# MLP, output projection and first gate as seven block products for eight

## The chip, the cores and the metric

The kernel runs on one core of one Trainium2 chip. The metric is device time in microseconds, from runs of the whole kernel. A core has TensorE (matrix products, PE in the profile), VectorE (DVE), ScalarE (ACT), GpSimd (POOL) and SyncE (SP, which here only issues DMAs).

## The reference

Two layers on 1024 tokens of width 1024, in float32. Each layer normalises h, projects it, runs eight heads of forgetting attention and eight of chunkwise retention, and then:

```python
        h = h + mixed @ w_out[i]                                  # 1024 x 1024
        h = h + gated_conv_ffn(rms_norm(h, ffn_norm_w[i]), w_up[i], conv_w[i], conv_b[i], w_down[i])
        gate = jax.nn.sigmoid(rms_norm(h, ple_norm_w[i]) @ w_ple_gate[i])   # 1024 x 1024
        h = h + gate * (p[i] @ w_ple_proj[i])
...
def gated_conv_ffn(u, w_up, conv_w, conv_b, w_down):
    up = u @ w_up                                                 # 1024 x 5632
    a, g = up[..., :D_FF], up[..., D_FF:]                         # D_FF = 2816
    a = causal_depthwise_conv(a, conv_w, conv_b)                  # three taps along the tokens
    return (jax.nn.gelu(a, approximate=False) * g) @ w_down       # 2816 x 1024
```

A final norm follows the second layer.

## The kernel before

Activations lie with features on the 128 partitions and the 1024 tokens along the free axis, so h is eight tiles of 128 x 1024. Each float32 operand is split into a high and a low part of reduced mantissa (`split`: ScalarE writes the high part, VectorE or GpSimd subtracts it from the source). A product of a 128 x 128 block of weights with 512 tokens is three matrix products: high by high, high by low, low by high (`mm_fm`, L163 and L165, two halves of the tokens, so six for a block).

Weights come one load of 512 KB ahead of their use (`load_w`, `fetch`, `weights`; tags wr, wh and wl with two buffers each), in the order that `weight_order` writes out by hand. The engine that makes a low part is read from the strings in `ENGINES`.

A layer runs in this order. First the attention stage: `weave` mixes dense products with attention units by spans written out by hand. Then the output projection: eight column chunks of eight blocks each; h[m] gains the result from PSUM (L738), `make_u` splits the scaled h[m] for the MLP, and its squares join the sum for the norm (`Stats`). Then the MLP: `up` takes one chunk of 128 of the 2816 features, convolves, applies gelu and multiplies with its gate; after every second chunk `down` adds that pair's product into all eight h tiles, by halves of 512 tokens (L780). Then the gate: eight chunks, whole for the first layer, by two pieces of 512 tokens for the last (L847 to L849), with the final norm behind them. `finish` turns the sums of squares into 1 / rms, by small products.

One SBUF pool `sb` and one PSUM pool `ps` serve the whole kernel; tags give the number of buffers (`BUFS`). PSUM has two double banks "d" and four single banks "s". Order on each engine comes from the framework's scheduler, which takes the program order as priority and a timing model of its own for what is ready.

## Time and profile before

| | us |
|---|---|
| median of 3 runs | 2913.52 |
| lowest and highest | 2911.53, 2914.69 |
| span of the profiled execution | 2907.6 |

The span runs from the first to the last instruction of one profiled execution; the run's time holds 5.9 us more at its median. Busy shares are those of the span. In rows, `x2048` counts instructions, `128x512` is partitions by elements, and "idle before" is the idle time of that engine just before such an instruction, with what ended it. A matrix product's own duration overlaps with its neighbours', so the pace is read from start to start. In windows, each engine's busy time is followed by its instruction count; PEclk is the granted TensorE clock as a share of 2.4 GHz.

### The profile page before, as it was taken

The numbers are of one execution on the slowest core, as the hardware profiler recorded it, in microseconds if no ns is written. First come the engines' busy times: TensorE is split into PE (matmuls) and PEld (weight loads), VectorE is DVE, ScalarE is ACT, GpSimd is POOL, SyncE is SP. The second block draws the span as 40 slices with busy tenths as digits, with TensorE's granted clock in tenths as the row PEclk, the third lists the DMA queues.
The fourth block names the chain that finished last, engine by engine and source line by source line (L and its number), as shares of the span: only waits on it lengthen the run. The fifth ranks groups of instructions, "written<-read, shape, count | busy, mean of one in ns | idle before, by whom it ended". The sixth has DMA issues, their size and how long they took to land. (4 is left out here: it accounts for less than half of the span.)

```text
span 2907.6 us, 35602 instructions
## 1 busy us (share of the span) xinstructions
PE 2855.6 (98%) x14654; PEld 2414.9 (83%) x14654; DVE 1559.9 (54%) x2343; ACT 936.6 (32%) x1312; POOL 363.3 (12%) x317
## 2 busy tenths in 40 slices
PE   9999999999999999999999999999999999999998
PEld 8888889888888888888888888888888888888876
DVE  4566655544444445446636666645344445444477
ACT  4455533421211212123435545243221211111243
POOL 2222332200000000000122222321000000000011
PEclk9999999999999999999999999999999999999999
DMA  5234222311111111112343341233111111111123
GB/s 167 83 86 107 57 69 75 141 47 48 51 44 51 46 49 51 44 51 80 117 113 83 88 109 32 71 109 110 44 51 44 51 44 51 47 49 46 60 85 137
DMA packets 70226, 209.79 MB, mean 72 GB/s; under 512 B 8624, under 2 KB 13232, under 8 KB 70064
## 3 DMA queue, kind: packets, MB, share of 16 engines
q1 hardware_dynamic: 66992, 199.12, 22.3%
q10 hardware_dynamic: 3072, 8.39, 1.2%
q8 instruction: 115, 1.88, 0.3%
q14 instruction: 47, 0.39, 0.0%
HBM read 157.09 MB, written 16.84 MB: 60 GB/s over the span
## 5 line engine op out<-in xcount | busy, mean ns | idle before, releaser
L163 PE MATMUL d<-uh,wh 128*128 128x512 f32 x2048 | 644.9, 395 | 0.3 <-ACT uh L100 0.3
L165 PE MATMUL d<-uh,wl 128*128 128x512 f32 x2048 | 639.5, 393 | 2.6 <-POOL wl L97 2.5
L163 PE MATMUL d<-ul,wh 128*128 128x512 f32 x2048 | 640.3, 393 | 0.6 <-DVE ul L101 0.6
L96 ACT CAST wh<-wr 128x1024 fp32r<-128x1024 f32 x232 | 243.2, 1049 | 1117.9 <-PE d L163 611.3
L165 PEld LDWEIGHTS d<-uh,wl 128*128 128x128 f32 x2048 | 384.3, 188 | 88.6 <-POOL wl L97 4.2
L163 PEld LDWEIGHTS d<-ul,wh 128*128 128x128 f32 x2048 | 384.4, 188 | 85.9 <-DVE ul L101 1.0
L163 PEld LDWEIGHTS d<-uh,wh 128*128 128x128 f32 x2048 | 381.3, 188 | 80.9 <-ACT uh L100 0.5
L780 DVE TENSOR_TENSOR h<-s,h 128x512 f32<-128x512 f32 x352 | 233.5, 686 | 173.4 <-PE s L165 171.7
L163 PE MATMUL s<-zh,wh 128*128 128x512 f32 x704 | 258.7, 394 | 0.0
L165 PE MATMUL s<-zh,wl 128*128 128x512 f32 x704 | 258.2, 394 | 0.0
L163 PE MATMUL s<-zl,wh 128*128 128x512 f32 x704 | 258.0, 393 | 0.0
L97 DVE TENSOR_TENSOR wl<-wr,wh 128x1024 fp32r<-128x1024 f32 x176 | 215.9, 1227 | 43.4 <-ACT wh L96 34.8
L183 PE MATMUL d<-wh,uh 128*128 128x256 f32 (+1 forms) x768 | 222.6, 290 | 11.7 <-DVE ks L332 8.6
L184 PE MATMUL d<-wl,uh 128*128 128x256 f32 (+1 forms) x768 | 220.6, 287 | 0.1
L185 PE MATMUL d<-wh,ul 128*128 128x256 f32 (+1 forms) x768 | 219.4, 287 | 0.0
L753 DVE TENSOR_TENSOR a<-d,rb 128x1024 f32<-128x1024 f32 x44 | 53.9, 1224 | 261.0 <-PE d L165 243.0
L762 DVE TENSOR_TENSOR z<-d,rb 128x1024 f32<-128x1024 f32 x44 | 53.9, 1225 | 246.2 <-PE d L165 246.2
L97 POOL TENSOR_TENSOR wl<-wr,wh 128x1024 fp32r<-128x1024 f32 (+1 forms) x56 | 137.4, 2455 | 354.4 <-ACT wh L96 241.1
L752 POOL MEMSET a<- 128x2 f32 x44 | 4.4, 100 | 1386.7 <-DVE zl L97 1268.3
L183 PEld LDWEIGHTS d<-wh,uh 128*128 128x128 f32 x768 | 147.2, 192 | 16.0 <-DVE ks L332 10.3
L165 PEld LDWEIGHTS s<-zh,wl 128*128 128x128 f32 x704 | 132.3, 188 | 31.1
L163 PEld LDWEIGHTS s<-zl,wh 128*128 128x128 f32 x704 | 132.4, 188 | 30.6
(196 smaller groups left out, 4202.0 us busy)
## 6 DMA issues: line engine op xcount, KB each, us to landing
wr<-in_wup_dram SPq DMA_DIRECT2D x88, 512.0 KB, 3.5
wr<-in_wdown_dram SPq DMA_DIRECT2D x44, 512.0 KB, 3.6
wr<-in_wqk_dram SPq DMA_DIRECT2D x32, 512.0 KB, 3.5
wr<-in_wgate_dram SPq DMA_DIRECT2D x24, 512.0 KB, 3.6
wr<-in_wtm_dram SPq DMA_DIRECT2D x20, 512.0 KB, 3.7
ka<-kh SPq DMA_DIRECT2D x32, 256.0 KB, 4.9
kb<-kl SPq DMA_DIRECT2D x32, 256.0 KB, 5.2
yb<-cum_rows SPq DMA_DIRECT2D x16, 512.0 KB, 5.1
```

What stands on the lines that cost most here:

```text
L96: nc.scalar.copy(dst_hi, src)
L97: (eng or nc.vector).tensor_tensor(dst_lo, src, dst_hi.bitcast(F32), op=ALU.subtract)
L163: nc.tensor.matmul(outs[h], whi, x[:, h * 512:(h + 1) * 512], start=s, stop=False)
L165: nc.tensor.matmul(outs[h], wlo, xhi[:, h * 512:(h + 1) * 512], start=False, stop=stop)
L183: nc.tensor.matmul(o, x[k][0][:, tok], hi, start=start, stop=False)
L184: nc.tensor.matmul(o, x[k][0][:, tok], lo, start=False, stop=False)
L185: nc.tensor.matmul(o, x[k][1][:, tok], hi, start=False, stop=stop)
L752: nc.gpsimd.memset(a[:, 0:2], 0.0)
L753: nc.vector.tensor_tensor(a[:, 2:], ad, rb, op=ALU.mult)
L762: nc.vector.tensor_tensor(z, gd, rb, op=ALU.mult)
L780: nc.vector.tensor_tensor(hs, outs[i], hs, op=ALU.add)
```

## The change

The output projection, both parts of the MLP and the gate of the first layer are computed by Strassen's form, in Winograd's variant, with blocks of two by two: weights in four blocks of 128 x 128 (two halves of a pair of K chunks, two halves of a pair of output chunks), activations in four blocks of 128 x 512 (two K chunks, two halves of the tokens). Seven block products, named b0, a, b1, c1, b2, c2 and b3, replace eight. Three PSUM banks hold them: b goes on adding to its bank after each reading out, as does c2 to c1's.

`Moving` holds a pair of activation chunks: the parts that are used as they are and four sums (`sums`), each split in high and low. `Fixed` holds a unit of weights (n pairs of K chunks, one pair of output chunks): GpSimd makes four sums, ScalarE and VectorE split seven blocks; `Line` loads one unit ahead and `parts` spreads its four steps over the products of the unit before. `join` adds block products to h, `form` builds a new tile.

The output projection runs in two halves of K, so units of n = 2. The MLP runs in two stages: all 22 chunks go up, in units of n = 4, and z and its sums go to DRAM (`zd`); then h is read again and the pairs of chunks come back in four groups, units of n = 3, 3, 3 and 2. Pools are opened by stage (`turn_to`): a tile of a new pool waits for the tiles of the old one that lay in its memory, and PSUM in the MLP stages is eight single banks. The last gate is as before, but its weights and `make_u` start in a new pool, as do those of the next attention stage.

```diff
+GROUPS = ((0, 1, 2), (3, 4, 5), (6, 7, 8), (9, 10))
...
-    sb = ctx.enter_context(tc.tile_pool(name="sb", bufs=1))
-    ps = ctx.enter_context(tc.tile_pool(name="ps", bufs=1, space=PSUM))
...
-    BUFS = dict(st=6, tp=5, L=4, c=3, u=16, mh=9)
+    BUFS = dict(st=6, tp=5, L=4, c=2, u=16, mh=9, ssq=1, x=28, wr=4, ws=2, wh=4, wl=3)
+    KEPT = ("mh", "ssq")
+    sb = ps = banks = None
+    @contextmanager
+    def phase(name):
+        nonlocal sb, ps, banks
+        banks = 8 if name[:3] == "ffn" else 4
+        with ExitStack() as stack:
+            sb = stack.enter_context(tc.tile_pool(name="sb_" + name, bufs=1, reuse_waits="tile"))
+            ps = stack.enter_context(tc.tile_pool(name="ps_" + name, bufs=1, space=PSUM, reuse_waits="tile"))
+            yield
...
+            yield from (None, None)
+            for i in range(len(PIECES) if l + 1 == DEPTH else 0):
+                yield from [(ap["wlast"][0, m], KC, P, E("gate%d" % l, i * KC + m)) for m in range(KC)]
...
+    class Moving:
+        def __init__(self, a, b, scales=None, ta=None, tb=None):
+            a1, b1, b2 = a[:, 0:512], b[:, 0:512], b[:, 512:T]
+            if ta is None:
+                ta, tb = sums(a, b, scales)
+            self.x = []
+            for n, (src, scale) in enumerate(((a[:, 0:512], scales and scales[0]), (b[:, 0:T], scales and scales[1]),
+                                              (ta.rearrange("p c t -> p (c t)"), None), (tb.rearrange("p c t -> p (c t)"), None))):
+                if n == 0:
+                    t = G("x", "xs", F32R, (P, 2, 512))
+                    hi, lo = t[:, 0, :], t[:, 1, :]
+                else:
+                    hi, lo = G("x", "xh", F32R), G("x", "xl", F32R)
+                if scale is None:
+                    split(hi, lo, src)
+                else:
+                    split_scaled(hi, lo, src, scale)
+                self.x.append((hi, lo))
+        def of(self, part):
+            n, slot = ((0, 0), (1, 0), (2, 0), (2, 1), (3, 0), (1, 1), (3, 1))[part]
+            return [v[:, slot * 512:(slot + 1) * 512] for v in self.x[n]]
+    def sums(a, b, scales=None):
+        a1, a2, b1, b2 = a[:, 0:512], a[:, 512:T], b[:, 0:512], b[:, 512:T]
+        ta, tb = G("c", "ta", F32, (P, 2, 512)), G("c", "tb", F32, (P, 2, 512))
+        t2, t1, t3, t4 = ta[:, 0, :], ta[:, 1, :], tb[:, 0, :], tb[:, 1, :]
+        if scales:
+            sa, sbb, sn = scales
+            nc.scalar.activation(t3, a2, AF.Copy, scale=sa)
+            nc.vector.scalar_tensor_tensor(t1, a1, sa, t3, op0=ALU.mult, op1=ALU.subtract)
+            nc.vector.scalar_tensor_tensor(t3, b2, sbb, t3, op0=ALU.mult, op1=ALU.subtract)
+        else:
+            sn = -1.0
+            nc.vector.tensor_tensor(t1, a1, a2, op=ALU.subtract)
+            nc.vector.tensor_tensor(t3, b2, a2, op=ALU.subtract)
+        nc.vector.scalar_tensor_tensor(t2, b2, sn, t1, op0=ALU.mult, op1=ALU.subtract)
+        nc.vector.scalar_tensor_tensor(t4, b1, sn, t2, op0=ALU.mult, op1=ALU.subtract)
+        return ta, tb
+    class Fixed:
+        def __init__(self, src, n, loads):
+            self.n, self.w = n, n * P
+            self.raw = []
+            for i in range(2):
+                t = G("wr", "wr", F32, (P, 2, self.w))
+                loads.append(nc.sync.dma_start(t, src[i]))
+                self.raw.append(t)
+            self.x = []
+            self.todo = [self.first, self.second, self.third, self.fourth]
+        def step(self):
+            if self.todo:
+                self.todo.pop(0)()
+        def split(self, t, c=2):
+            if c == 2:
+                hi, lo = G("wh", "wh", F32R, (P, 2, self.w)), G("wl", "wl", F32R, (P, 2, self.w))
+            else:
+                both = G("wh", "wb", F32R, (P, 2, self.w))
+                hi, lo = both[:, 0:1, :], both[:, 1:2, :]
+            nc.scalar.copy(hi, t)
+            nc.vector.tensor_tensor(lo, t, hi.bitcast(F32), op=ALU.subtract)
+            self.x.append((hi, lo))
+        def first(self):
+            self.split(self.raw[0])
+        def second(self):
+            (a, b), s = self.raw, G("ws", "ws", F32, (P, 2, self.w))
+            nc.gpsimd.tensor_tensor(s[:, 1, :], b[:, 0, :], b[:, 1, :], op=ALU.add)
+            nc.gpsimd.tensor_tensor(s[:, 0, :], s[:, 1, :], a[:, 0, :], op=ALU.add)
+            self.p = s
+            self.split(s)
...
+        def take(self):
+            now = self.ahead
+            while now.todo:
+                now.step()
+            self.load()
+            return now
...
+    def parts(line, moving, evac):
+        w = line.take()
+        b, c = bank(), None
+        for part, name in enumerate(("b0", "a", "b1", "c1", "b2", "c2", "b3")):
+            if name == "a":
+                o = bank()
+            elif name == "c1":
+                o = c = bank()
+            else:
+                o = c if name == "c2" else b
+            more = name in ("b1", "b2", "b3", "c2")
+            for p, x in enumerate(moving):
+                whi, wlo = w.of(part, p)
+                xhi, xlo = x.of(part)
+                first, last = p == 0 and not more, p == len(moving) - 1
+                nc.tensor.matmul(o, whi, xhi, start=first, stop=False, skip_group_check=more)
+                nc.tensor.matmul(o, whi, xlo, start=False, stop=False, skip_group_check=more)
+                nc.tensor.matmul(o, wlo, xhi, start=False, stop=last, skip_group_check=more)
+            evac(name, o)
+            if part in (1, 3, 5, 6):
+                line.step()
+    def join(name, s, to):
+        c11, c12, c21, c22 = to[0][:, 0:512], to[0][:, 512:T], to[1][:, 0:512], to[1][:, 512:T]
+        for dst, op in {"b0": [(c11, ALU.add)], "a": [(c11, ALU.add)], "b1": [(c12, ALU.add)], "c2": [(c12, ALU.add)],
+                        "c1": [(c22, ALU.subtract)], "b2": [(c22, ALU.subtract)], "b3": [(c21, ALU.subtract)]}[name]:
+            nc.vector.tensor_tensor(dst, dst, s, op=op)
+    def form(name, s, to, scale):
+        c11, c12, c21, c22 = to[0][:, 0:512], to[0][:, 512:T], to[1][:, 0:512], to[1][:, 512:T]
+        if name in ("b0", "b1"):
+            nc.scalar.copy(c11 if name == "b0" else c12, s)
+        elif name == "c1":
+            nc.scalar.activation(c22, s, AF.Copy, scale=-1.0)
+        elif name in ("a", "c2"):
+            dst = c11 if name == "a" else c12
+            nc.vector.tensor_tensor(dst, dst, s, op=ALU.add)
+        elif name == "b2":
+            nc.vector.tensor_tensor(c22, c22, s, op=ALU.subtract)
+        else:
+            nc.vector.scalar_tensor_tensor(c21, s, -1.0, scale, op0=ALU.mult, op1=ALU.mult)
...
+        line = Line(specs())
+        h = [None] * KC
+        stats = Stats()
+        u = []
+        hs_dram = dr.tile([KC, P, T], F32, name="hs")
+        mx = [Moving(mixed[2 * p], mixed[2 * p + 1]) for p in range(4)]
+        for half in range(2):
+            for q in range(4):
+                if half == 0:
+                    for m in (2 * q, 2 * q + 1):
+                        h[m] = G("mh", "h")
+                        with tc.issue_after(line.loads[0].ins):
+                            nc.sync.dma_start(h[m], h_dram[m])
+                to = h[2 * q:2 * q + 2]
+                parts(line, mx[2 * half:2 * half + 2], lambda name, s: join(name, s, to))
+                if half:
+                    u.append(Moving(*to, scales(2 * NW_FFN + l, q)))
+                    for m in (2 * q, 2 * q + 1):
+                        stats.add(h[m], G("mh", "hsq"))
+                        nc.sync.dma_start(hs_dram[m], h[m])
+        zd = [dr.tile([4, P, T], F32, name="zd%d" % j, bufs=1) for j in range(FC // 2)]
+        rb = None
+        for j in range(FC // 2):
+            act = []
+            body = [G("mh", "a") for i in range(2)]
+            def evac_a(name, s):
+                nonlocal rb
+                if rb is None:
+                    _, rb = stats.finish()
+                form(name, s, body, rb[:, 0:512])
+                if name == "b2":
+                    nc.vector.tensor_tensor(body[1][:, 512:T], body[1][:, 512:T], rb[:, 512:T], op=ALU.mult)
+                elif name == "c2":
+                    nc.vector.tensor_tensor(body[0], body[0], rb, op=ALU.mult)
+            parts(line, u, evac_a)
...
+                for tap in (1, 0):
+                    late = c[:, 2 - tap:T]
+                    nc.vector.scalar_tensor_tensor(late, body[i][:, 0:T - 2 + tap], cw[:, tap:tap + 1], late, op0=ALU.mult, op1=ALU.add)
+                nc.scalar.activation(c, c, AF.Gelu)
+                nc.vector.tensor_tensor(c, c, rb, op=ALU.mult)
+                act.append(c)
...
+            parts(line, u, evac_g)
+            ta, tb = sums(*z)
+            for n, t in enumerate((z[0], z[1], ta.rearrange("p c t -> p (c t)"), tb.rearrange("p c t -> p (c t)"))):
+                nc.sync.dma_start(zd[j][n], t)
...
+        for group in GROUPS:
+            mx = []
+            for j in group:
+                t = []
+                for n, shape in enumerate(((P, 512), (P, T), (P, 2, 512), (P, 2, 512))):
+                    t.append(G("c" if n else "mh", "zz", F32, shape))
+                    src = zd[j][n]
+                    if n == 0:
+                        src = src[:, 0:512]
+                    elif n > 1:
+                        src = src.rearrange("p (c t) -> p c t", c=2)
+                    nc.sync.dma_start(t[-1], src)
+                mx.append(Moving(t[0], t[1], ta=t[2], tb=t[3]))
+            u = []
+            for q in range(4):
+                to = h[2 * q:2 * q + 2]
+                parts(line, mx, lambda name, s: join(name, s, to))
+                if group is GROUPS[-1]:
+                    if l + 1 < DEPTH:
+                        u.append(Moving(*to, scales(2 * NW_PLE + l, q)))
+                    for m in (2 * q, 2 * q + 1):
+                        stats.add(h[m], G("mh", "hsq"), None, E("hsq", m))
...
+            turn_to("attn%d" % (l + 1))
+            fetch()
...
+    turn_to("last")
+    fetch()
+    fetch()
+    u = [make_u(h[m], nw[:, 2 * NW_PLE + DEPTH - 1, m:m + 1]) for m in range(KC)]
```

Left out: comments; `third` and `fourth` of `Fixed` (two more sums by GpSimd, the last two splits); `evac_g` (as `evac_a`, with the activated half as scale); the gate of the first layer (four units of n = 4 by `parts` and `form`, the product with the embedding on GpSimd); the new layout of the weights on the host. In the attention stage `cs` takes the `ssq` buffer.

## Rows read from the trace of the kernel before

**Rows 1.** The page, part 1: busy time, share of span, instructions, by engine.

```profile
PE 2855.6 (98%) x14654; PEld 2414.9 (83%) x14654; DVE 1559.9 (54%) x2343; ACT 936.6 (32%) x1312; POOL 363.3 (12%) x317
```

**Rows 2.** Busy time by stage: window, length, engines, PEclk, DMA share, GB/s.

```profile
545.00:634.00 89.00, 88.45 (x384) 70.86 (x383) 39.12 (x33) 26.79 (x27) 5.52 (x3) 1.00 0.17 54
634.00:1362.00 728.00, 728.00 (x3177) 594.86 (x3178) 362.06 (x385) 159.77 (x150) 6.26 (x23) 1.00 0.15 50
1362.00:1460.00 98.00, 98.00 (x445) 80.88 (x444) 60.88 (x47) 40.06 (x39) 17.54 (x7) 1.00 0.35 118
...
1985.00:2073.00 88.00, 87.47 (x385) 70.43 (x384) 38.06 (x32) 27.45 (x27) 5.33 (x3) 1.00 0.18 54
2073.00:2803.00 730.00, 729.39 (x3177) 595.23 (x3177) 364.80 (x385) 161.08 (x150) 11.05 (x25) 1.00 0.16 50
2803.00:2907.00 104.00, 90.16 (x441) 74.96 (x439) 73.13 (x106) 36.17 (x51) 16.99 (x9) 0.95 0.38 129
```

**Rows 3.** TensorE, groups of instructions by form.

```profile
L163 PE MATMUL d<-uh,wh 128*128 128x512 f32 x2048 | 644.9, 395 | 0.3 <-ACT uh L100 0.3
...
L163 PE MATMUL s<-zh,wh 128*128 128x512 f32 x704 | 258.7, 394 | 0.0
...
L163 PE MATMUL d<-mxh,wh 128*128 128x512 f32 x256 | 80.2, 397 | 1.0 <-DVE h L738 1.0
```

**Rows 4.** The last gate: TensorE by time, then busy sums of 2825 to 2885.

```profile
2842.78 0.39 PE L848 MATMUL d<-ul,wh 128*128 128x512 f32 x1
2843.01 0.39 PE L849 MATMUL d<-uh,wl 128*128 128x512 f32 x1
...
sum 60.00, PE 60.00 PEld 49.34 DVE 48.32 ACT 23.88 POOL 11.18; mean PE 10.00 PEld 8.22 DVE 8.05 ACT 3.98 POOL 1.86
```

**Rows 5.** VectorE in order of time: joins of MLP down, then the first gate.

```profile
698.63 1.88 DVE L780 TENSOR_TENSOR h<-s,h 128x512 f32<-128x512 f32 x3
...
1438.31 1.22 DVE L97 TENSOR_TENSOR wl<-wr,wh 128x1024 fp32r<-128x1024 f32 x1
1439.44 1.28 DVE L101 SCALAR_TENSOR_TENSOR ul<-h,nw,uh 128x1024 fp32r<-128x1024 f32 x1
1440.63 1.22 DVE L811 TENSOR_TENSOR sg<-sg,ppt 128x1024 f32<-128x1024 f32 x1
```

**Rows 6.** ScalarE, groups of instructions by form.

```profile
L96 ACT CAST wh<-wr 128x1024 fp32r<-128x1024 f32 x228 | 238.9, 1049 | 1102.0 <-PE d L163 607.3 <-PE s L163 356.7 <-issue 117.3
...
L411 ACT CAST pth<-s 128x512 fp32r<-128x512 f32 x96 | 56.1, 585 | 59.0 <-PE s L409 58.4
```

**Rows 7.** GpSimd, groups of instructions by form.

```profile
L97 POOL TENSOR_TENSOR wl<-wr,wh 128x1024 fp32r<-128x1024 f32 x52 | 127.7, 2456 | 319.9 <-ACT wh L96 224.5 <-issue 72.8 <-DVE sg L855 15.8
...
L348 POOL TENSOR_TENSOR yb<-yb,triangle 128x128 f32<-128x128 f32 x128 | 66.7, 524 | 334.6 <-DVE mn L363 259.3 <-DMA yb<-cum_rows 55.6 <-DVE fsum L370 19.6
```

**Rows 8.** GpSimd and VectorE in order of time, at 1362 and 2781 us.

```profile
1362.03 2.93 POOL L97 TENSOR_TENSOR wl<-wr,wh 128x1024 fp32r<-128x1024 f32 x1 [16.46 <-ACT wh L96]
...
1362.62 3.43 DVE L230 TENSOR_TENSOR ssq<-ssq,hsq 128x1024 f32<-128x1024 f32 x1
...
2781.14 2.56 POOL L230 TENSOR_TENSOR ssq<-ssq,hsq 128x1024 f32<-128x1024 f32 x1 [69.11 <-ACT hsq L229]
...
2781.35 1.37 DVE L780 TENSOR_TENSOR h<-s,h 128x512 f32<-128x512 f32 x2
```

**Rows 9.** DMA issues: count, KB each, median us from issue to landing.

```profile
wr<-in_wup_dram SPq DMA_DIRECT2D x88, 512.0 KB, 3.5
...
pp<-ppt SPq DMA_DIRECT2D x16, 512.0 KB, 2.9
...
ppt<-pp SPq DMA_DIRECT2D x8, 512.0 KB, 5.3
```

**Rows 10.** Busy time by windows, columns as above, in the second attention stage.

```profile
1745.00:1755.00 10.00, 5.07 (x37) 4.79 (x37) 8.11 (x18) 4.34 (x7) 6.47 (x6) 0.96 0.20 66
1755.00:1765.00 10.00, 9.04 (x58) 7.86 (x56) 7.67 (x23) 7.50 (x18) 1.83 (x4) 0.87 0.00 0
```

213 lines of the change are left out of this document (103 added, 110 removed).

## The prediction

> **What bounds the kernel now.** I read four views. First the busy shares [rows 1]: TensorE works 2855.6 of a span of 2907.6 us, so all its idle time is 52 us; VectorE is at 54%, ScalarE at 32%, GpSimd at 12%. Then the span by stages [rows 2]: in the output projection, both MLPs and the first gate (545 to 1460 and 1985 to 2803) TensorE is busy in all but a microsecond or so, at granted clock 1.00 (its level of 2.4 GHz). The idle 52 us lie in the attention stages and behind 2803, which the change leaves as they are. In the MLP 3177 products take 728 to 730 us, so one starts every 0.230 us (the 394 ns of [rows 3] is one product's own, pipelined duration). VectorE is busy there 50%, and nothing else is near a limit. So time falls only if products go away, and whatever is added to the other engines is free while TensorE never waits for it. The question is whether the new work stays under that cover.
>
> **What goes.** [rows 3], each shown for one of its three kinds of product: 3 x 2048, of which 3 x 512 belong to query and key chunks (32 chunks x 8 x 6), so 4608 for MLP up and first gate; 3 x 704 = 2112 for MLP down; 3 x 256 = 768 for the output projection. Together 7488, all 512 columns wide. Seven of eight stay: 936 go, 936 x 0.230 = 215.3 us. Would the pace hold, with another stationary block in every third product? The last gate before has just this order (high by high, high by low, low by high, one half of the columns) and starts a product each 0.23 us [rows 4]. So I take 0.230. A unit of `parts` is then 7 x 3 x n products: 9.66 us for n = 2, 14.5 for n = 3, 19.3 for n = 4.
>
> **Prices.** VectorE passes 512 columns in 1.88/3 = 0.63 us, starts a 1024-column operation each 1.13 and a scaled one of that size 1.19 us after its start [rows 5]; ScalarE takes 1.05 us for 1024 and 0.585 for 512 columns [rows 6]. GpSimd's additions of 256 to 512 columns are not in the trace; 128 columns take 0.52 and 1024 take 2.46 us [rows 7], a line through both gives 0.80, 1.08 and 1.35 us for 256, 384 and 512.
>
> **MLP up, 44 units of 19.3 us.** VectorE per unit: low parts of seven weight blocks 3 x 1.13 + 0.63 = 4.0; reading out 5 x 0.63 + 1.13 = 4.3; convolution and its product, per pair of units 2 x (2 x 1.19 + 1.13) = 7.0, so 3.5; sums of z 4 x 0.63 per pair, so 1.3. In all 13.1 us, 68%. ScalarE: 3 x 1.05 + 0.585 for the weights, three copies of 0.585, and four passes of 1024 columns per pair, at some 1.1: 7.7 us. In the last gate TensorE stayed full with VectorE at 80% (48.3 of 60 us, [rows 4]). Only b2 is read out by VectorE ahead of a product that adds to the same bank, with c2's 2.8 us between. I take 6 us for both layers, between 0 and 40.
>
> **Output projection, 16 units of 9.66 us.** Here the cover fails. In the second half VectorE has per unit: seven joins 4.4, the next weights 2.2, the new `Moving` of two rows of h (sums 4 x 0.63, splits 0.63 + 1.19 + 2 x 1.13) 6.6, squares 2.3: 15.5 us against 9.66. That is 5.8 us short in each of four units, 23; some 5 of it lie beside the first MLP unit. In the first half the first two `Moving` need 2 x (2.5 + 1.13) = 7.3 us before b1, and b0 and a cover 2.8: 4.5 us; the rest of that half is 42 us of VectorE against 38.6, 3 more. With 4 us for GpSimd's hold on VectorE [rows 8] it is 30 us a layer, 60 in both. Ends: 36 in both, if the start is covered by the embedding's products and half of the lack by reordering; 100, if the joins, which stand behind the `Moving` on VectorE and which TensorE waits for, come late on top.
>
> **Start of MLP down.** z comes back through two buffers of tag c; no x tile is free before the last up unit ends. A buffer's turn is a load of 512 KB, 3.5 us (2.9 to 5.3, [rows 9]), the high part 1.05, the low part 1.22 and hand-offs of some 0.4: 6.2 us. The first group has nine such tiles, so five turns in one buffer, and the first turn starts about 5.5 us after the last product (read-out, sums, their DMA of 2.9 us): the last tile is there at 36.5 us, and 21 products, 4.8 us, still follow. The unit ends at 41.3 instead of 14.5: 27 us lost a layer, 54 in both (40 with the fastest load, 76 with the slowest). SP holds the next weights behind the waiting loads; they are due one unit later and late by nothing. At the second and third group one `Moving` fits ahead, two tiles wait in c, and four are a turn late: 4.5 us each, 18 in all (0 to 40). The h loads lie before these in SP's queue and are counted in the start.
>
> **MLP down itself.** For n = 3 VectorE has per group three `Moving` 12, weights 12 and joins 18: 42 of 58 us. I take 8 us for both layers (0 to 45). The last group of the first layer has the lack of the output projection again, as it builds the gate's `Moving`: 4 x 5.8 less 5 beside the gate, 20 us with rounding up for its own loads (8 to 40). In the last layer it doesn't.
>
> **Ends of stages, attention, clock.** Before, the splits for the next attention and the last gate ran beside the products; now they wait until the x tiles in whose memory they lie are free, and the first weights until their pool opens: eight splits at 1.19 us with some six under products. 8 us at the attention, 6 at the last gate (0 to 30 together). Attention has the same buffers of `c` and `ssq` together: 0 (-5 to 10). The clock: after a stretch in which TensorE was busy 5.07 of 10 us it was at 0.87 for the next 10 [rows 10], that is 2.6 us at 1.2 GHz and 1.3 us lost. Two waits of 27 us: 4 us (0 to 10).
>
> **Sum.** 60 + 6 + 54 + 18 + 8 + 20 + 14 + 4 = 184 us come back of 215.3. 2907.6 - 215.3 + 184 = 2876; the median of the runs, 2913.5, lies 5.9 us above the profiled span, so 2882.
>
> **A rule against the change.** When GpSimd and VectorE both read SBUF, the trace shows VectorE held: a sum of squares took 3.43 us for 1.2 beside a GpSimd operation of 2.93; two joins out of PSUM beside one of 2.56 took 0.69 each, as always [rows 8]. The Trainium skill ("SBUF — State Buffer", section "SBUF: two separate sides") says why: GpSimd and VectorE share a pair of ports as an exclusive lock, held for the whole instruction, and VectorE needs it with two SBUF inputs. By that rule, the trace agrees, the splits, sums and convolutions are exposed and the joins aren't; with every GpSimd microsecond on the path it would be the first rival below, at its far end.
>
> **Rivals.** (1) Slower: VectorE becomes the bound through GpSimd's new additions, four in each unit. 48 units x 4 x 1.35 + 24 x 4 x 1.08 + 24 x 4 x 0.80 = 440 us are new, in stages where GpSimd is now idle [rows 2]. For: [rows 8]; up then has 13.1 + 5.4 = 18.5 of 19.3 us, down 10.5 + 4.3 = 14.8 of 14.5. Against: a third of VectorE's work there reads PSUM, and TensorE has up to 2.8 us of patience. If one in four of these microseconds ends in a wait of TensorE, 110 us more: 2992. It decides (no gain left) from 31 us, one in fourteen. (2) Much faster: reordering hides what I count, z's return at its fast end. With all low ends, 36 + 40 + 8 + 0, the sum is 84: 2782; with some of the rest, up to 2835. For: before, TensorE stays full across every stage end [rows 2]. Against: VectorE's 15.5 us for 9.66 is a rate, and no order changes it. (3) The change does not do what it says: the pace gets worse by a seventh, to 0.263 us, with the stationary changes. Then 2882 + 215 = 3097. [rows 4] speak against it.
>
> **Numbers.** Forecast 0.50 (its own range 2835 to 2920), (1) 0.28, (2) 0.20, (3) 0.02. Range: low 2795, leaving out a part of (2); high 2990, leaving out some half of (1). This kernel's three runs lie within 3.2 us, so 0.2%, 5.8 us, is no change. Faster: all of (2) and 0.42 of the forecast, 0.62; same: 0.06; slower: 0.32.
>
> **What would show it.** 6552 products of this kind at 0.230 us; TensorE's idle time some 230 us for 52, in two stretches of 25 to 30 us where MLP down starts, in the second half of each output projection and in the first layer's last down group, with VectorE above 90% there. In MLP up TensorE over 98% busy. Wrong: waits of TensorE in every up unit with VectorE's SBUF operations lengthened (rival 1); no long gap at the start of down (rival 2); a pace other than 0.230 (rival 3).

## The result, and the profile after

The changed kernel takes 2931.31 us (median of 4 runs, 2928.44 to 2932.09), beside 2912.53 (2908.84 to 2914.69) for the kernel before: a ratio of 1.0061, 95% interval 1.0047 to 1.0075. It is slower by 0.6%, some 18.8 us. The forecast was 2882 us, faster by 1%; its direction was wrong, and the measured time lies inside the range. The spans of the two profiled executions, by which everything below is counted, differ by 22.7 us. The 4 us between that and 18.8 are chance: a run's time holds 1.8 us more than its span here, so the profiled execution of the kernel before lay some 3 us below its median and this one 1 above. Of the 5.9 us that the forecast added for the runs, some 4 were such chance.

The busy shares (page, part 1; answers to [rows 1]):

```profile
PE 2699.2 (92%) x13718; PEld 2272.5 (78%) x13718; DVE 2085.0 (71%) x2991; ACT 1216.3 (42%) x1778; POOL 918.5 (31%) x650
```

TensorE works 156 us less, and the profiled span of 2930.3 us leaves it idle 231 us, as the forecast had it ("some 230"). But the span grew by 22.7 us. The agreement is luck: a part of the products ran at half the clock, and a product that takes 0.39 us at the full clock is listed there as 0.63 us of busy time. So the idle time alone doesn't tell the loss, and I read the profile by places. First the pace of the products that stay (TensorE in order of time, MLP up; start, duration):

```profile
800.13 0.39 PE L351 MATMUL q<-xl,wb 128*128 128x512 f32 x1
...
800.59 0.39 PE L350 MATMUL q<-xh,wb 128*128 128x512 f32 x1
...
801.04 0.39 PE L352 MATMUL q<-xh,wb 128*128 128x512 f32 x1
```

Four products in 0.91 us. Over MLP up the mean from start to start is 0.2267 us, where the same count of the kernel before gives 0.2303 (0.230 in the forecast, [rows 2, 4]). The pace got better: 6552 x 0.0036 = 24 us that I hadn't forecast (norm products and waits are left out of both means).

Then the busy time by places (columns as in [rows 2]), both layers, each window from the last product of one place to the last of the next: output projection, first unit of MLP up, rest of MLP up, first quarter of the first group of MLP down, the rest with two groups, the last group, the gate; then the second layer, whose last window holds all the rest of MLP down:

```profile
543.00:642.00 99.00, 85.32 (x338) 63.77 (x337) 97.38 (x138) 50.36 (x70) 43.66 (x33) 0.95 0.37 118
642.00:685.00 43.00, 30.05 (x118) 24.31 (x117) 31.22 (x32) 15.36 (x19) 13.04 (x7) 0.72 0.22 73
685.00:1090.00 405.00, 401.98 (x1764) 331.74 (x1762) 338.47 (x322) 161.77 (x194) 151.50 (x86) 1.00 0.33 114
1090.00:1135.00 45.00, 24.56 (x67) 15.71 (x68) 21.82 (x26) 16.02 (x19) 2.04 (x2) 0.66 0.74 243
1135.00:1295.00 160.00, 158.08 (x693) 129.60 (x693) 121.36 (x154) 58.27 (x73) 50.31 (x45) 1.00 0.42 130
1295.00:1350.00 55.00, 41.19 (x166) 31.23 (x164) 52.83 (x65) 27.38 (x36) 23.55 (x18) 0.96 0.22 63
1350.00:1470.00 120.00, 90.32 (x368) 72.64 (x368) 68.18 (x68) 41.97 (x50) 36.57 (x18) 0.85 0.21 70
...
2021.00:2120.00 99.00, 85.87 (x337) 63.87 (x337) 97.36 (x137) 50.47 (x70) 43.59 (x33) 0.95 0.38 118
2120.00:2163.00 43.00, 30.09 (x117) 24.63 (x118) 30.88 (x32) 15.02 (x19) 13.03 (x7) 0.72 0.21 73
2163.00:2568.00 405.00, 401.78 (x1763) 331.58 (x1762) 338.85 (x323) 161.96 (x194) 151.38 (x86) 1.00 0.33 114
2568.00:2613.00 45.00, 24.22 (x66) 15.53 (x67) 21.33 (x25) 15.86 (x19) 1.89 (x2) 0.66 0.72 241
2613.00:2813.00 200.00, 196.25 (x859) 160.41 (x858) 154.12 (x200) 73.78 (x95) 61.07 (x56) 1.00 0.39 120
```

A window's length less its products at 0.2267 us is what was lost there. The counts are known from the code (336, 84, 1764, 63, 693, 168, 336, and 924 for all of MLP down); the x of the rows holds the norm's instructions too, and those that a window's edge cuts.

| place | forecast, us | lost in the trace, us |
|---|---|---|
| output projections | 60, a part of it beside the next unit | 2 x 22.8 = 46 |
| first units of MLP up | (in the 60) | 2 x 24.0 = 48 |
| rest of MLP up | 6 | 2 x 5.1 = 10 |
| start of MLP down | 54 | 2 x 30.7 = 61 |
| group boundaries, down itself | 18 + 8 | 2.9 + 4.8 = 8 |
| last group, first layer | 20 | 17 |
| gate | 0 | 44 |
| ends and starts of attention | 8 | 35 |
| last gate | 6 | 5 |
| clock | 4 | no term of its own (below) |
| sum | 184 | 274 |

The attention's 35 us are worked out from the two traces. From the end of the first gate's last product to that of the second output projection's it is 613.0 us before (1448.3 to 2061.3) and 649.8 after (1469.9 to 2119.7). In the trace before nothing parts the gate from the dense products behind it, so its last product is taken as the 3552nd behind the projection (3168 of the MLP, 384 of the gate); it can't lie behind 1450.0, where VectorE begins to read it out:

```profile
1450.02 1.22 DVE L809 TENSOR_TENSOR sg<-d,rb 128x1024 f32<-128x1024 f32 x1
```

Of the growth of 36.8, the projection's own part is 22.8 lost less 12.2 saved, and 26 stay. The same sum for the first layer leaves 8.5. The gate's row is 0 because the 20 of the forecast were all put beside the last group.

The sum closes. 274, less some 11 that the kernel before lost in the same places by the same count, less the 24 of the pace, is 239; the products that went were worth 215.3, and 215.3 + 22.7 is 238. This checks the bookkeeping and not the causes, as the attention's row is itself a remainder.

Two views show what the lost places have in common. The waits of TensorE, by what ended them (instruction, releaser; sum, times, longest):

```profile
PE q L350 <- ACT xs L112: 34.9, 6, 13.0
PE s L404 <- DVE ssq L395: 29.0, 4, 11.7
PE q L350 <- DVE h L362: 25.5, 19, 4.3
PE s L733 <- DVE yn L728: 14.0, 3, 7.1
...
PE s L404 <- DVE fr L488: 9.0, 1, 9.0
PE q L351 <- DVE xs L117: 8.9, 2, 4.5
...
PE q L350 <- ACT sg L368: 6.6, 2, 6.4
...
PE s L418 <- POOL rc L407: 3.9, 2, 3.7
```

The first line is the reload of z at the start of MLP down. The second is the norm's sum of squares, the third the joins, the fourth the end of each attention, the fifth the norm ahead of the second attention, and the last two belong to the gate. And VectorE in order of time at the start of the first MLP up:

```profile
643.07 1.97 DVE L113 TENSOR_TENSOR xl<-tb,xh 128x1024 fp32r<-128x1024 f32 x1
644.96 1.74 DVE L117 SCALAR_TENSOR_TENSOR xs<-h,nw,xs 128x512 fp32r<-128x512 f32 x1
...
649.55 2.29 DVE L395 TENSOR_TENSOR ssq<-ssq,hsq 128x1024 f32<-128x1024 f32 x1
651.77 1.74 DVE L249 SCALAR_TENSOR_TENSOR ta<-h,nw,tb 128x512 f32<-128x512 f32 x1
...
657.09 1.21 DVE L395 TENSOR_TENSOR ssq<-ssq,hsq 128x1024 f32<-128x1024 f32 x1
```

From 560 to 663 us it is busy 101.4 of 103. With TensorE beside it:

```profile
641.90 0.40 PE L350 MATMUL q<-xs,wh 128*128 128x512 f32 x1
646.75 0.80 PE L351 MATMUL q<-xs,wh 128*128 128x512 f32 x1 [4.45 <-DVE xs L117]
...
649.91 0.63 PE L352 MATMUL q<-xh,wb 128*128 128x512 f32 x1
658.36 3.58 PE L404 MATMUL s<-ones,ssq 128*128 128x1 f32 x16 [7.82 <-DVE ssq L395]
661.79 0.77 PE L350 MATMUL q<-xs,wh 128*128 128x512 f32 x1
```

TensorE waits 4.45 us for the last low part, then 7.82 us in order for a sum that no product behind it needs yet. The products between and behind start every 0.43 us in place of 0.227: the granted clock is at 1.2 GHz. Over the whole span the mean clock is 0.958, so (1 - 0.958) x 2 x 2930 = 246 us were spent at that level, beside some 30 before. That gave the first theory.

### The profile page after: what moved, and what is told of

Read it like the earlier page. It is cut to its first block, busy times and chain, and to the rows that moved or that the text cites. A ratio compares the mean times of both kernels' runs of the same rounds, so it can differ in the third digit from the quotient of the medians.

```text
span 2930.3 us, 36348 instructions
## 1 busy us (share of the span) xinstructions
PE 2699.2 (92%) x13718; PEld 2272.5 (78%) x13718; DVE 2085.0 (71%) x2991; ACT 1216.3 (42%) x1778; POOL 918.5 (31%) x650
## 5 line engine op out<-in xcount | busy, mean ns | idle before, releaser
L350 PE MATMUL q<-xh,wh 128*128 128x512 f32 x1560 | 617.3, 398 | 30.6 <-DVE h L362 16.4
L351 PE MATMUL q<-xl,wh 128*128 128x512 f32 x1560 | 615.1, 394 | 3.9 <-DVE xl L113 3.9
L352 PE MATMUL q<-xh,wl 128*128 128x512 f32 x1560 | 604.6, 394 | 0.0
L350 PEld LDWEIGHTS q<-xh,wh 128*128 128x128 f32 x1560 | 297.4, 191 | 112.3 <-DVE h L362 26.2
L292 POOL TENSOR_TENSOR ws<-wr 128x512 f32<-128x512 f32 (+2 forms) x96 | 143.4, 1494 | 715.5 <-DVE wl L284 596.2
L351 PEld LDWEIGHTS q<-xl,wh 128*128 128x128 f32 x1560 | 296.9, 190 | 69.7 <-DVE xl L113 9.5
L352 PEld LDWEIGHTS q<-xh,wl 128*128 128x128 f32 x1560 | 297.1, 190 | 62.4 <-DVE wl L284 0.6
L299 POOL TENSOR_TENSOR ws<-wr 128x512 f32<-128x512 f32 (+2 forms) x96 | 121.8, 1269 | 308.7 <-DVE wl L284 308.7
L162 PE MATMUL d<-uh,wh 128*128 128x512 f32 x512 | 166.7, 403 | 1.1 <-ACT wh L112 0.7
L162 PE MATMUL d<-ul,wh 128*128 128x512 f32 x512 | 163.4, 396 | 0.6 <-DVE ul L117 0.6
L164 PE MATMUL d<-uh,wl 128*128 128x512 f32 x512 | 161.3, 395 | 2.7 <-POOL wl L113 2.5
```

What stands on the lines that cost most here:

```text
L162: nc.tensor.matmul(outs[h], whi, x[:, h * 512:(h + 1) * 512], start=s, stop=False)
L164: nc.tensor.matmul(outs[h], wlo, xhi[:, h * 512:(h + 1) * 512], start=False, stop=stop)
L350: nc.tensor.matmul(o, whi, xhi, start=first, stop=False, skip_group_check=more)
L351: nc.tensor.matmul(o, whi, xlo, start=False, stop=False, skip_group_check=more)
L352: nc.tensor.matmul(o, wlo, xhi, start=False, stop=last, skip_group_check=more)
```

## The experiments

Fourteen kernels. Theory 1: the waits are as forecast, but the low clock behind each of them halves the pace of products that nothing else holds (TensorE was busy in 148 of the 246 us, in 20 before; half of the difference is 64 us, for 4 forecast). Theory 2: the low clock costs nothing, since what runs behind a wait waits for VectorE too. Theory 3: GpSimd's new additions hold VectorE, the prediction's first rival. What a place lost is counted in each kernel as above.

**e1_fill**, products of ones by ones in the waits.

```
+ def fill(n):
+     s = spsum()
+     with tc.issue_after(last_mm[0].ins):
+         for i in range(n):
+             nc.tensor.matmul(s[:, 0:P], ones, ones, start=True, stop=True)
```

> Products of ones by ones (128x128, nobody reads them) are put in order on TensorE in its longest waits: 14 inside the first block product of MLP up, 32 or 50 or 36 ahead of the norm's products (MLP up, first gate, second attention), 14 behind them in the gate, 52 and 16 at the start of MLP down; 334 in all. They do no work of the kernel. Theory 1 (the waits lower the clock, and the products bound by TensorE behind each wait then run at half pace, about 64 us in all): the time at 1.2 GHz falls from 246 us to under 150 and the kernel comes to 2880 to 2905 us. Theory 2 (the low clock costs nothing, the products behind a wait are waiting for VectorE anyway): the time stays within 2925 to 2940 whatever the clock does. Theory 3 (VectorE held by GpSimd's additions): no change, 2925 to 2940.

2953.48 us, ratio 1.0142 (1.0126 to 1.0157): 22 us slower than the changed kernel, outside what any theory expected; the time at 1.2 GHz fell to 171 us, not under 150. In most places the fillers came in between products that could have run, and held them up (the first unit of MLP up lost 30.5 us for 24). One place is a clean test, the start of MLP down, where they nearly fitted into the wait (the first product behind them starts 14.4 us after MLP up, for 13.4). Busy time from the last product of MLP up to the end of the first quarter:

```profile
1097.00:1142.00 45.00, 36.39 (x200) 28.64 (x199) 21.47 (x25) 15.02 (x18) 0.42 (x2) 0.85 0.71 237
```

The clock is 0.85 for 0.66, that is 13.5 us at 1.2 GHz in place of 30.6, 17 less, and the stretch is 45 us long in both. The Trainium skill ("TensorE: Matmul & The Clock Gate", section "Terms") prices time at the low level at half of it; an estimate by that is 8.5 us for the 17. The 17 us were worth next to nothing: from the first of the 63 products behind the wait to the last it takes 30.7 us for 31.1, since they stood waiting for the splits of z, whose loads come in turn, at either level. At this place theory 1 is out.

**e2_finish**, the norm's products later.

```
-                 if rb is None:
+                 if rb is None and name == "b2":
                      _, rb = stats.finish()
...
-             if name == "qs":
+             if name == ("ks" if l else "qs"):
                  rc, rb = stats.finish()
```

> The norm's products (which need the sum of squares, the last thing that VectorE makes) are issued later, behind the fifth block product of the first unit of MLP up and of the gate, and behind the second dense product of the second attention, in place of the first: TensorE, which takes its instructions in order, no longer stands before them (29 us of waits in the trace of the changed kernel). Theory 1: the 29 us and, with the waits, a part of the low clock behind them: 2870 to 2898. Theory 2: the 29 us alone at best, and part of it comes back as waits for the moving halves: 2900 to 2920. Theory 3: within 0.3% of 2931.

2913.13 us, ratio 0.9998 (0.9989 to 1.0008), 18 us faster than the changed kernel. That is theory 2's number. The first units of MLP up lose 18.9 us for 24: a wait of 7.89 for the next moving half stands where the wait of 7.82 for the sum had been, so the order cost 5 us, and VectorE's queue the rest.

**e3_groups**, groups of 2, 3, 3, 3.

```
- GROUPS = ((0, 1, 2), (3, 4, 5), (6, 7, 8), (9, 10))
+ GROUPS = ((0, 1), (2, 3, 4), (5, 6, 7), (8, 9, 10))
```

> The groups of MLP down are 2, 3, 3, 3 units in place of 3, 3, 3, 2: a shorter reload and split ahead of the first product of MLP down (six split tiles fewer on VectorE's queue per unit left out), and a longer last group under which the moving halves of the gate are made. Theory 1: about 5 us less wait at the start of each MLP down and some 10 to 15 at the end of the first, and half as much again from the clock: 2895 to 2915. Theory 2: the waits alone, 2908 to 2922. Theory 3: within 0.3% of 2931.

2912.18 us, ratio 0.9998 (0.9988 to 1.0008), 19 us faster: inside what theories 1 and 2 both expected, so it doesn't tell them apart. The first quarter of MLP down lost 23.2 and 26.4 for 30.7, the last group of the first layer 10.0 for 17.

**e4_nopool**, without GpSimd's additions: the blocks themselves are split in place of their sums, so the products are of other numbers.

```
-             nc.gpsimd.tensor_tensor(s[:, 1, :], b[:, 0, :], b[:, 1, :], op=ALU.add)
-             nc.gpsimd.tensor_tensor(s[:, 0, :], s[:, 1, :], a[:, 0, :], op=ALU.add)
-             self.p = s
-             self.split(s)
+             self.split(self.raw[1])
```

> GpSimd's four additions per weight tile are left out: the raw blocks are split in place of their sums, so that the products are of other numbers; instructions on TensorE, VectorE and ScalarE are as many as before. Theory 3 (GpSimd's new additions hold VectorE, and with it TensorE): MLP up and the output products lose their waits, 2860 to 2890. Theories 1 and 2 (the additions are hidden): 2915 to 2932, at most some us at the starts of stages where VectorE is the one that ends last.

2902.35 us, ratio 0.9963 (0.9950 to 0.9976): 29 us faster than the changed kernel, between what the theories expected. Its busy shares, then, each for the changed kernel and for this one, the sums of squares on VectorE (shortest, median, longest, ns) and the joins:

```profile
PE 2694.8 (93%) x13718; PEld 2274.7 (78%) x13718; DVE 1945.5 (67%) x2991; ACT 1217.6 (42%) x1778; POOL 349.6 (12%) x266
```

```profile
L395 DVE TENSOR_TENSOR ssq<-ssq,hsq x26: 1206/1210/2291, 615.7 to 2814.5; 128x1024 f32<-128x1024 f32 x26
L388 DVE TENSOR_TENSOR ssq<-ssq,hsq x26: 1208/1218/1226, 615.2 to 2785.9; 128x1024 f32<-128x1024 f32 x26
```

```profile
L362 DVE TENSOR_TENSOR h<-h,q 128x512 f32<-128x512 f32 x336 | 225.2, 679 | 69.1 <-PE q L352 67.0
L355 DVE TENSOR_TENSOR h<-h,q 128x512 f32<-128x512 f32 x336 | 226.7, 683 | 81.2 <-PE q L345 79.7
```

GpSimd works 569 us less (the prediction's estimate was 440) and VectorE, with as many instructions, 140 us less; no sum is stretched any more. The joins, which read PSUM, are as long in both: they were not held, which the prediction had expected. One microsecond in four of GpSimd's additions held VectorE. At most one in twenty reached the end, as the run also spares the splits their wait for the additions. Some 100 of the 140 us lie in MLP up, where VectorE falls from 84% to 72% and TensorE hardly waits: in the rest of MLP up the loss falls from 5 us a layer to about 1. The first rival is real, but small.

After these four I put the cause otherwise. Theory V: at the start and end of each stage the end of VectorE's queue decides, and the clock beside it is a sign, not a price.

**e5_nosum**, without the seven additions of each sum of squares in the MLP pools; the norms are of other numbers.

```
-                 (eng or nc.vector).tensor_tensor(self.ssq[:, c], self.ssq[:, c], room, op=ALU.add)
+                 if not leave:
+                     (eng or nc.vector).tensor_tensor(self.ssq[:, c], self.ssq[:, c], room, op=ALU.add)
```

> In the two output projections, at the end of the two MLPs and in the first gate the sum of squares is left out: the squares are made, but only the first row's stays (7 additions of 1.13 us less each time, on VectorE; the norms are of other numbers). Theory V (new, after the first four kernels: at the starts of the stages the end of VectorE's queue decides, and the low clock beside it costs nothing): each of these microseconds is one of TensorE's: about 8 us less in the first unit of each MLP up, 8 to 16 in and behind the first gate, 2 to 5 at the last gate, 2893 to 2908. Theory 1 (the low clock costs): the same waits shorten, and the time at 1.2 GHz with them, 2885 to 2905, with more gained than the 8 us in a place. If VectorE isn't what ends last there: 2924 to 2932.

2878.54 us, ratio 0.9884 (0.9869 to 0.9899): 53 us faster, more than any theory expected, for 35 additions of 1.13 us, 40 us. The first unit of MLP up:

```profile
639.00:670.00 31.00, 26.03 (x107) 18.88 (x106) 24.74 (x28) 15.99 (x20) 11.36 (x8) 0.94 0.27 98
```

It takes some 30 us in place of 43: 13 us for 7.9 us of additions. VectorE's work in these places is TensorE's time, and more than one to one. The surplus of 5 us may be the squares' room, GpSimd's hold or the norm at half pace; this run can't separate them.

**e6_wout8**, the output projection in eight products, with its pairs of MLP up made late.

```
-                 to = h[2 * q:2 * q + 2]
-                 parts(line, mx[2 * half:2 * half + 2], lambda name, s: join(name, s, to))
+             outs = eight(ready, mx)
+             for i in range(2):
+                 c = slice(i * 512, (i + 1) * 512)
+                 nc.vector.tensor_tensor(h[m][:, c], h[m][:, c], outs[i], op=ALU.add)
```

> The output projection goes back to eight products of 128x512 for seven (8 splits of the mixed rows in place of the sums of four pairs, two joins a row in place of seven twice a unit); MLP and gate stay. Only one of four moving pairs of MLP up can be made before its end, since the eight rows' halves hold the x tiles. Theory V: 96 products a layer come back, 22 us, and the 23 us that the trace shows lost inside the projection go to about 8, while the first unit of MLP up loses 24 us as before or a little more: 2930 to 2955, that is, seven products gain nothing in the projection. Theory 1: TensorE is busy without a wait up to the end of the projection, and the clock with it: 2895 to 2920.

2900.86 us, ratio 0.9959 (0.9944 to 0.9974): 30 us faster. Theory 1's number fits; theory V's own, 2930 to 2955, was wrong, and in direction. 48 products a layer came back, not the 96 of the expectation: 10.9 us. Output projection, then first unit of MLP up:

```profile
543.00:636.00 93.00, 89.49 (x386) 73.70 (x386) 56.95 (x60) 37.73 (x41) 9.00 (x6) 0.96 0.40 139
636.00:670.00 34.00, 27.67 (x119) 22.61 (x118) 20.49 (x22) 12.42 (x16) 8.43 (x5) 0.85 0.14 47
```

VectorE has 57 us of work for 97. The projection loses 6 us for 23, and the first unit 15 for 24, although three of its four pairs are made only then: VectorE comes to them with an empty queue. That is V's mechanism, read after the fact: my expectation had left that queue out.

**e7_gate8**, the first gate in eight products.

```
-                 parts(line, u, evac_s)
+                 outs = eight(ready, u)
+                 if m == 0:
+                     _, rb = stats.finish()
```

> The first gate goes back to eight products; output projection and MLP stay. In the last group of the first MLP down VectorE makes 8 scaled splits (1.19 us each) in place of four moving pairs (6.6 us each). 48 products come back, 11 us. Theory V: of the 17 us lost in the last group some 12 go, and of the 44 lost in and around the gate about half: 2895 to 2912. Theory 1: the same and the clock, 2885 to 2905. If neither the moving halves nor the norm is what bounds there: 2935 to 2943.

2892.53 us, ratio 0.9933 (0.9917 to 0.9950): 39 us faster, 2.5 us more than V's range and inside theory 1's. Last group of MLP down, then the gate:

```profile
1294.00:1334.00 40.00, 39.24 (x170) 31.15 (x169) 36.62 (x50) 20.04 (x26) 11.80 (x11) 1.00 0.26 73
1334.00:1431.00 97.00, 93.87 (x417) 77.30 (x415) 42.47 (x46) 29.21 (x29) 18.41 (x8) 0.96 0.31 103
```

The last group loses 2 us for 17, the gate (384 products, 87 us) 9 to 10 for 44. So 50 us went, for 10.9 us of products.

**e8_keep**, MLP down begins with the last two units, the last z straight from SBUF.

```
- GROUPS = ((0, 1, 2), (3, 4, 5), (6, 7, 8), (9, 10))
+ GROUPS = ((9, 10), (0, 1, 2), (3, 4, 5), (6, 7, 8))
...
+                 if j == FC // 2 - 1:
+                     mx.append(Moving(*z, ta=ta, tb=tb))
+                     continue
...
-                     t.append(G("c" if n else "mh", "zz", F32, shape))
+                     t.append(G("c" if n and j != GROUPS[0][0] else "mh", "zz", F32, shape))
```

> MLP down begins with the last two units: z of the last stays in SBUF and is split from there, z of the one before is loaded through free tiles of the other tag, so that no load through the two buffers of tag c stands ahead of the first products; the groups are then three of three. Theory V: 30 us lost in the first quarter of each first group become 12 to 20 (two pairs of 4.1 us of splits and the last sums, for three with their loads in turn), and the last group of the first layer, of three now, loses some 7 us less: 2885 to 2905. Theory 1: the same waits, and half as much again from the clock: 2870 to 2890. If the loads' turn isn't the cause: 2920 to 2931.

2882.36 us, ratio 0.9893 (0.9878 to 0.9908): 49 us faster, 2.6 us more than V's range and inside theory 1's. The first quarter of MLP down, 42 products now:

```profile
1090.00:1106.00 16.00, 12.41 (x43) 8.60 (x43) 15.74 (x21) 8.38 (x11) 1.82 (x3) 0.89 0.87 304
```

16 us, 6.5 lost for 30.7. A group of two alone had left 23 to 26 (e3_groups), so some 17 to 20 are the loads and their turn through two buffers, as the prediction had it. VectorE is full here (15.74 of 16, for 21.8 of 45 before): what is left is its splits. The rest of that group, of two units, now loses 3 to 4 us a layer for none.

By numbers theory V does badly: all four kernels came out faster than its ranges, while theory 1's held in three. So the totals don't decide between the two; the places do. What a place lost went where VectorE's queue or the loads went. Whether the clock has a price beside that needs fillers that hold nothing up (e12 to e14).

**e9_all**, e6, e7 and e8 in one.

> The last three of the kernels before in one: output projection and first gate with eight products, MLP in seven with the last unit's z kept in SBUF (groups 2, 3, 3, 3; five of the gate's eight splits wait for the last group's tiles). Theory V: the losses stand in different places and add up: 30 + 39 + 49 us less than the changed kernel's 2931, some 8 less for the last group, which two of them mend, and some 6 for the late splits: 2818 to 2832, faster than before by 3%. If the places give their gain to the next wait: above 2850.

2812.29 us, ratio 0.9657 (0.9643 to 0.9670). 119 us below the changed kernel, where the three alone gave 30 + 39 + 49 = 118: the losses stood in different places and add up, but for the last group of MLP down, which e7 and e8 both mend. That is 6 us below the numbers expected. It is faster than before by 3.4%. Output projection, first unit, first quarter of MLP down, gate:

```profile
543.00:637.00 94.00, 90.49 (x388) 74.44 (x388) 57.37 (x60) 38.08 (x41) 8.99 (x6) 0.95 0.41 138
637.00:671.00 34.00, 27.69 (x118) 22.62 (x117) 20.14 (x22) 12.08 (x16) 8.43 (x5) 0.80 0.13 47
1073.00:1090.00 17.00, 12.91 (x46) 8.82 (x45) 16.13 (x22) 9.05 (x13) 1.88 (x4) 0.90 0.79 293
1297.00:1392.00 95.00, 93.02 (x416) 77.69 (x414) 37.91 (x40) 26.68 (x26) 18.41 (x8) 0.96 0.27 95
```

**e10_all**, the same with groups of 3, 3, 3, 2 that begin with the last three units.

```
+ GROUPS = ((8, 9, 10), (0, 1, 2), (3, 4, 5), (6, 7))
```

> As the kernel with all three, but the groups are 3, 3, 3, 2 with the last three units first: three pairs of moving halves stand ahead of the first unit's end (4.1 us more of VectorE, and one more load through tag c), while the units of the first group have 14.5 us for the joins and the gate's splits find free tiles early. Theory V: 5 us more in the first quarter of MLP down and 4 to 6 less in the rest of the group, each layer, and some 6 less at the gate: 2812 to 2830.

2821.47 us, ratio 0.9690 (0.9676 to 0.9703): inside the numbers expected, but 9 us above e9_all. Its first quarters lose 10 us for 7, MLP up 5 us a layer for 2, and the last group of two costs 2 us a layer where that of three costs none; the rest of the groups gives some 4 us a layer back. The profiled spans differ by 5.8 us (2819.5 and 2813.7).

**e11_lazy**, e9_all with the norm's products later, as in e2_finish, in MLP up and the second attention.

> As the kernel with all three, and the norm's products stand behind the fifth block product of MLP up and behind the second dense product of the second attention. TensorE isn't stopped in order by the sum of squares. Theory V: 3 to 5 us less in each first unit of MLP up, 0 to 9 less ahead of the attention: 2805 to 2822, 6 to 15 below the kernel with all three.

2806.76 us, ratio 0.9635 (0.9622 to 0.9649), 5.5 us below e9_all, just short of the 6 to 15 expected. The first units lose 10.1 us for 15. At the attention nothing changed: the norm still ran ahead of the dense products, behind the same wait of 8.32 us.

**e12_fill**, e9_all with 24 fillers in the one wait at the start of MLP up.

> As the kernel with all three, and 24 products of ones by ones (0.23 us each in the earlier trace) in the one wait of 5 to 6 us at the start of each MLP up (ahead of the fourth moving pair of the first block product). Behind this wait TensorE ran 8.5 us of products and the norm at 1.2 GHz with no wait between them. Theory 1, now for this place alone: with the clock kept, 4 us less in each layer, 8 below the kernel with all three. Theory 2 (the low clock costs nothing here either): the same time within 2 us, or some us more where the fillers end late.

2808.12 us, ratio 0.9638 (0.9625 to 0.9651), 4 us below e9_all, between the theories. The first unit, beside e9_all's second row above:

```profile
636.00:670.00 34.00, 32.35 (x168) 27.86 (x167) 20.89 (x23) 12.63 (x17) 8.45 (x5) 0.90 0.13 47
```

6.8 us at 1.2 GHz for 13.6, and the unit loses 14.4 us for 15.0 in this layer, 14.4 for 14.7 in the other. The clock fell all the same, 0.2 us after the norm's narrow products began and behind two waits of 1.2 and 0.4 us that were left. Of the 5.9 us between the two profiled spans, 2.5 lie in the second attention, which the edit doesn't touch, and the rest in parts of one at most. This doesn't show a price of the clock, and doesn't exclude one.

**e13_fillgate** and **e14_lazyfill**, 36 fillers behind the gate's last product in e9_all and in e11_lazy, where the norm and ten dense products had run at half pace with hardly a wait.

```
+            idle = spsum()
+            with tc.issue_after(latest[0].ins):
+                for i in range(36):
+                    nc.tensor.matmul(idle[:, 0:P], ones, ones, start=True, stop=True)
```

> As the kernel with all three (output projection and first gate in eight products, the last z kept), and 36 products of ones by ones stand behind the last product of the first gate, in the one wait of 8.3 us ahead of the norm's products. Theory 1, for this place: the norm's two sets (3.57 and 3.79 us at 1.2 GHz) and the ten dense products between and behind them run at full pace; from the end of the gate's products to the first dense ones at full pace 20.1 us become some 15, and the time falls by 5 us. Theory 2: the rows after the wait take as long as before, since they wait for the row of the norm and the weights; no change within 2 us.

> The same 36 products in the kernel with all three and the later norm, which has the same wait and the same 17.1 us at 1.2 GHz behind it. Theory 1: 5 us below that kernel, about 2802. Theory 2: the same as that kernel, 2805 to 2809.

2810.51 us, ratio 0.9652 (0.9639 to 0.9666), and 2804.39 us, ratio 0.9630 (0.9617 to 0.9643): 1.8 and 2.4 us below their own bases. The 20 us behind the gate's last product, in e9_all and then in e13_fillgate:

```profile
1392.00:1412.00 20.00, 10.80 (x41) 9.22 (x40) 13.91 (x13) 13.03 (x14) 7.99 (x3) 0.59 0.49 153
```

```profile
1391.00:1411.00 20.00, 16.66 (x114) 15.79 (x113) 14.06 (x14) 13.51 (x14) 7.89 (x3) 0.83 0.51 167
```

16.4 us at 1.2 GHz become 6.8. The norm's first set takes 1.92 us for 3.57, but then TensorE waits 2.94 us for the norm's row, and the 20th dense product starts 22.2 us after the gate's end for 22.7 (21.3 for 22.6 in the other pair). Of the 5 us expected by theory 1, about one came by then. Up to its last product the whole attention takes 547.7 us for 551.5 and 548.9 for 552.2, where kernels with the same code there range from 548.9 to 551.5; so at most some 4 us are the fillers'. e14_lazyfill is the fastest kernel of this study, 3.7% below before; its lead on e11_lazy is not sure, and the two stood on different chips.

## Why the prediction was wrong

**The pace** of 0.230 us was to hold; it got better by 0.0036, 24 us on the good side, which was luck: without it the kernel would have been slower by some 1.5%. Rival 3 is out.

**MLP up** was right: 10 us for 6, TensorE at 402 of 405 us with VectorE at 84% (68% were worked out; without GpSimd's additions it is 72%, the rest is their hold). So was **MLP down**: its start 61 for 54, its boundaries and itself 8 for 26, the last group 17 for 20. e8_keep shows the mechanism of the start. Only the sign that VectorE would be above 90% there was wrong: it is busy in 21.8 of 45 us, and the loads decide.

**The output projection** is the first step that failed. The prediction counted VectorE 5.8 us short in each of the four units of the second half, let "some 5 of it lie beside the first MLP unit", and gave the first half 7.5 us. The projections lose 46 us for 60, but not in this way: counted by units, the first half loses 14.4 a layer (10.9 of it in its first unit), and the four units of the second half lose 0, 0, 2.5 and 5.9 in the first layer. The shortage isn't paid where it arises. VectorE stands a queue behind, and the next stage's unit hides nothing of it: it needs the last pair's low part at once, and in its order stands the norm, which needs the last square. That unit lost 24 us a layer. Together 94 us for 60. That this is near the far end of 100, which I had given for joins that come late, is chance: in the first projection and the unit behind it TensorE waits 5.9 us for joins. e2_finish, e5_nosum and e6_wout8 each take a part of the 24 away.

**The gate and the ends of stages** failed by more. I put a price on the gate's moving halves in the last group (17 for 20) and on the splits behind the gate (8), and none on the gate itself. It lost 44 us: four units behind a full VectorE queue with the norm in order (11.7 us), its row (3.7), and one wait of 6.4 for the two buffers that hold a unit's output. e7_gate8 removes 50 of these 61 us. The attention was put at 0 because its code is the same, and its ends at 8; the two traces lose 35 us there, 26 of them around the second attention. The norm ahead of it waits 9 us, and the second output projection doesn't begin beside the end of the attention any more. These are not the price of seven products: e9_all has as many products in projection and gate as the kernel before, and still takes 644.5 us from the end of the gate to the end of the second projection for 613.0, and 13.6 us more up to the end of the first projection. Of these 45 us its projections lose 12 themselves; some 33 stay at the edges of the attention. What is still different there is the division into stages, with their own pools and buffers. That is argued from the traces; no experiment took it apart.

**The clock** was 4 us. The time at 1.2 GHz is eight times what the kernel before had, and half of it would have explained the loss alone, so that was my first reading. The fillers speak against it: 0 us gained at the start of MLP down, 3 in the gate in e1_fill (41 lost for 44), about 1 ahead of the attention. No place behind a wait showed more than 3 us. Up to 5 us in the first units of MLP up stay open, and up to 4 over the whole second attention.

**Rivals.** The first one happens, at one microsecond of GpSimd's additions in twenty at most; 29 us is under the 31 from which it would have decided by itself. It isn't the cause, though without it the change would have gained 10 us. The second doesn't: z's return lost 61 us for 54, and only the group boundaries lost less than was counted.

So the failing step is the cover at the ends of stages. I costed VectorE's shortage inside a stage, took the next stage as a place to hide it, and put the gate at nothing. Seven products saved 11 us in a projection or in the gate, and cost 26 to 50 us there; in the MLP they saved 91 us a layer and cost 40, beside what projection and gate left to it.

## What to carry to other kernels

Saving one product in eight pays where a stage is long, because the price, more work on VectorE per unit, comes due at the stage's start and end. Count what the last unit of a stage leaves in VectorE's queue and what the first products of the next need from it; shortage that crosses the border is not hidden but waited for. A low granted clock beside a wait is to be tested before it is priced: fill the wait, and see whether the products behind it come earlier. And a change that also divides a kernel into stages has a second price: some 33 us at the edges of the attention are still there in e9_all.

## What the hardware showed that I had not expected

- Products of 512 columns start every 0.2267 us in the changed kernel and every 0.2303 in the kernel before, at the same clock. The seven block products aren't the reason: the eight products of e9_all's projection start every 0.2268, and those of the changed kernel's last gate, in the form before, every 0.2272. The reason stays open.
- 569 us of GpSimd's additions stretched VectorE's work by 140 us, more than half of it in three kinds of operation that read SBUF twice: the low parts of `wb` at 512 columns (1.39 us on average for 0.68 without the additions) and the first two sums of z (1.76 and 1.58 for 0.69). The joins, which read PSUM, took 0.68 in both.
- The norm's sixteen narrow records (128x1) took 3.57 us at 1.2 GHz and 1.92 us at 2.4 (e9_all, e13_fillgate).
